# Two inner tiles per SwiGLU step, in-place normalized tiles, a fifth weight buffer and a product moved to VectorE in a two-layer hybrid trunk

## The chip, the cores and the metric

The kernel runs on one core of a Trainium2 chip. The core has TensorE (PE, matrix products, with weight loads listed as PEld), VectorE (DVE), ScalarE (ACT), GpSimd (POOL) and SyncE (SP, which here only issues DMAs). The metric is the device time of one execution in microseconds (us), as the median of several runs.

## The reference

A trunk of two layers over one sequence of 256 positions, 1024 wide. Each layer is a SwiGLU feed-forward part, a mixer, and a second SwiGLU part; layer 0 mixes with RG-LRU and gated linear attention side by side, layer 1 with multi-head latent attention. Every part reads its input through a scale and shift computed from the conditioning vector c, and ends in a gated residual and a layer norm:

```python
def modulate(x, shift, scale):
    return x * (1 + scale[:, None, :]) + shift[:, None, :]

def deepnorm_residual(x, f, gate, g, b, weight=1.0):
    return layer_norm(DN_ALPHA * x + weight * (1 + gate[:, None, :]) * f, g, b)

def swiglu(u, w_in, w_out):
    gate, up = jnp.split(u @ w_in, 2, axis=-1)
    return (jax.nn.silu(gate) * up) @ w_out
...
    # rg_lru
    a = jnp.exp(log_a)
    u = jnp.sqrt(-jnp.expm1(2.0 * log_a)) * (i * x).astype(F32)
    _, h = lax.associative_scan(combine, (a, u), axis=1)
```

The inner width of SwiGLU is 2816, so w_in has 2 x 22 output tiles of 128 (22 gate, 22 up). All arithmetic is f32.

## The kernel before, in words

**Layout and precision.** Activations are kept transposed: a tile is 128 channels by 256 positions, and the 1024 channels are 8 tiles, indexed k. An f32 product is done as three fp32r matmuls on split operands: high·high (L407), low·high (L408) and high·low (L409). The activation u is therefore held as `uhi` and `ulo`, the inner activation of SwiGLU as `hhi` and `hlo`, and each weight as `whi` and `wlo`.

**Weight stream** (class `Stream`). All weight tiles (128x128) lie in the order of their use in slabs of 16 (1 MB). SP brings a slab into one of five `wraw` buffers; the tables of c's projections (`modw`) go through the same buffers. A slab is split in two halves of 8 tiles: ACT copies the half rounded to fp32r (`whi`, L338), DVE subtracts that copy from the raw weights (`wlo`, L339). When PE's program reaches half slab s, the splits up to s + AHEAD have been put into the program; `whi` and `wlo` have four buffers each and AHEAD is 3. One half slab feeds 24 matmuls. The projections of c are sums of products on DVE (`junk`, L388, 144 of them), dispersed among the splits.

**Boundary** (class `Boundary`, six of them, five with a successor). Each output tile of a part gets gate and residual on DVE (`yy`, L581) and its square on ACT; sums over the tiles are kept in `acc`. A correction (`shift`) is made from tile 0 once that is there: ACT rounds it, PE sums it over channels (L566), ACT copies the sum, and POOL subtracts it from seven residual tiles (`ax`, L571). Then mean and variance come from PE (L597 to L600), `center` subtracts the mean from a tile (DVE L603), and r is minus two over the standard deviation. While that runs, PE has the "early" products of the next part's first output tiles with the uncentred input held in two `flat` tiles (two to four output tiles of 8 x 3 matmuls). Then `u(k)` makes the next part's operand of tile k, one tile at a time: DVE multiplies by r (`ut`, L657), ACT adds the shift and rounds (`uhi`, L658), DVE subtracts (`ulo`, L659). Once u is done, `residual` makes the next residual `ax` in two steps, DVE L665 and ACT L666. `u` is called eight times in the first pass over k of the next part, one k per half slab or so.

**SwiGLU** (`ffn`). The first passes take several inner tiles j together over k; after them come the tail j's, one at a time with one bank for the gate and one for the up half. `glu(j)` is: silu on ACT into `sg`, product with the up half on DVE (`h`, L702), split into `hhi` (ACT L444) and `hlo` (DVE L445), each on a 128x256 tile.

**RG-LRU** (`rglru`, called for two groups of four channel tiles). Per tile a small gate weight `rgt` comes by a DMA on SP's queue (L829, two buffers); a convolution, two matmuls (L835, L836) and elementwise work follow, then for the group of four tiles a chain of 128x1024 operations on DVE, of which L850 is the last; POOL multiplies by the input (L851), and DVE runs four scans (L853).

**Order.** A scheduler places each engine's instructions in one fixed order by priorities (`tc.high_priority`) and data; each engine then runs its own list in order, and waits at an instruction whose operands or buffers aren't there.

Of the kernel before, what the change touches and what calls it, by code (L numbers as in the profile page):

```python
# [21 lines left out]
P = 128  # L22
# [32 lines left out]
FROW = 320  # L55
# [176 lines left out]
def trunk_kernel(ctx: ExitStack, tc: tile.TileContext, xT, cvec, pos, wst, modw, colsd,  # L232
# [6 lines left out]
    whi = ctx.enter_context(tc.tile_pool(name="whi", bufs=4))  # L239
# [3 lines left out]
    wlo = ctx.enter_context(tc.tile_pool(name="wlo", bufs=4))  # L243
# [31 lines left out]
    crow = T(wk, [1, DM], tag="junk", bufs=1)  # L275
# [24 lines left out]
    class Stream:  # L300
        RAW = 4
        HS = SLAB // 2
        AHEAD = 3
# [210 lines left out]
    class Boundary:  # L514
        def __init__(self, l, s, weight):
# [14 lines left out]
            if not self.last:  # L530
# [15 lines left out]
                self.ya = [flat(q, F32R).rearrange("p (k c) -> p k c", k=KD) for q in range(2)]  # L546
# [12 lines left out]
        def shift_out(self):  # L559
# [4 lines left out]
            act.activation(yr, y, AF.Copy)  # L564
# [29 lines left out]
        def stats(self, y, ysq):  # L594
# [7 lines left out]
            def center(k):  # L602
                vec.tensor_tensor(self.y[:, k, :], self.y[:, k, :], mean, SUB)  # L603

            odd_next = not self.last and self.next[1] == 1 and self.next[0] % 2
            with tc.high_priority(), tc.manual_schedule(engines={DVE, ACT}):
# [8 lines left out]
                for k in range(PRE):  # L615
                    center(k)
                r, rlast = rsqrt2(v, SEQ)
                self.r = r
                if self.last:
                    for k in range(KD):  # L620
                        self.normal(k, r)
                        if k + PRE < LPOOL:
                            center(k + PRE)
                    return
# [3 lines left out]
            self.center = center  # L628
# [4 lines left out]
            for m, f in early(*self.next):  # L633
                ps = mmps()
                for k in range(KD):
                    mm3(ps[:, :SEQ + 2], W.next((m, k, f)), [t[:, k, :SEQ + 2] for t in self.ya], k == 0, k == KD - 1)
# [7 lines left out]
            if odd_next:  # L644
                for k in range(PRE, KD):
                    center(k)

        def u(self, k):
# [4 lines left out]
            with tc.high_priority(offset=UOFF):  # L653
                if k >= PRE:
                    self.center(k)
                xa = T(wk, [P, SEQ], tag="ut")
                vec.scalar_tensor_tensor(xa, self.y[:, k, :], self.hA[:, k:k + 1], self.r, MULT, MULT)  # L657
                act.activation(uhi[:, k, :], xa, AF.Identity, bias=self.B[:, k:k + 1])  # L658
                vec.scalar_tensor_tensor(ulo[:, k, :], xa, self.B[:, k:k + 1], uhi[:, k, :].bitcast(F32), ADD, SUB)  # L659

        def residual(self, ks=range(KD)):
            W.pause = False
            for k in ks:
                xg = T(wk, [P, SEQ], tag="xh", bufs=3)
                vec.scalar_tensor_tensor(xg, self.y[:, k, :], self.ag[:, k:k + 1], self.r, MULT, MULT)  # L665
                act.activation(ax[:, k, :], xg, AF.Identity, bias=self.ab[:, k:k + 1])  # L666
# [24 lines left out]
    def ffn(l, i, prev):  # L691
        with tc.tile_pool(name=nm("ffn"), bufs=1) as fp:
# [4 lines left out]
            def glu(j, pg, pu, bg=0.0, bu=0.0, off=100):  # L697
                with tc.high_priority(offset=off):
                    sg = T(wk, [P, SEQ], tag="sg")
                    ta(sg, pg, AF.Silu, bias=bg)  # L700
                    h = T(wk, [P, SEQ], tag="h")
                    vec.scalar_tensor_tensor(h, pu, bu, sg, ADD, MULT)  # L702
                    split(h, hhi[:, j, :], hlo[:, j, :])

            for j in range(EARLY if prev else 0):
                (pg, bg), (pu, bu) = prev.values[2 * j:2 * j + 2]
                glu(j, pg, pu, bg, bu)

            passes = ffn_passes(l, i)
            part = {}  # L710
            for g, ks in passes:
                grp = {j: mmps() if q < 6 else axps() for q, j in enumerate(g)}
                for k in ks:
                    prev.u(k) if prev else first_u(k)
                    for j in g:
                        for half in range(2):
                            mm3(grp[j][:, half * SEQ:(half + 1) * SEQ], W.next((m, k, half * NJ + j)), u(k),
                                k == ks[0] and half == 0, k == ks[-1], True)
                if ks[-1] < KD - 1:
                    keep = [flat(q) for q in range(2)]  # L720
                for q, j in enumerate(g):
                    ps = grp[j]
                    if ks[-1] < KD - 1:
                        part[j] = keep[q // 4][:, (q % 4) * 512:(q % 4 + 1) * 512]
                        act.activation(part[j], ps, AF.Copy)
                        continue
                    off = GOFF
                    if j in part:
                        off -= GLATE * q
                        with tc.high_priority(offset=off):  # L730
                            vec.tensor_tensor(part[j], ps, part[j], ADD)  # L731
                        ps = part[j]
                    glu(j, ps[:, :SEQ], ps[:, SEQ:], off=off)
# [582 lines left out]
```

## Time and profile before

| what | value |
|---|---|
| median of 3 runs | 1037.29 us (1035.79 to 1043.17) |
| the profiled execution, its own time | 1033.83 us |
| its span in the profile | 1032.1 us |
| PE busy | 995.5 us, 96% of the span |
| DVE busy | 884.7 us, 86%, 1491 instructions |
| ACT busy | 612.5 us, 59%, 1023 instructions |
| POOL busy | 54.8 us, 5%, 72 instructions |
| granted TensorE clock | 0.996 of full speed |
| moved by DMA | 258.57 MB, mean 251 GB/s |

In a profile line, L339 is line 339 of the kernel; `wlo<-wraw,whi` reads "the tile wlo is made from wraw and whi"; xN counts instructions. A row of a timeline has start, duration, engine, line and operation, and in brackets the idle time before it with what ended that.

### The profile page before, as it was taken

The numbers are of one execution on the slowest core, as the hardware profiler recorded it, in microseconds if no ns is written. First come the engines' busy times: TensorE is split into PE (matmuls) and PEld (weight loads), VectorE is DVE, ScalarE is ACT, GpSimd is POOL, SyncE is SP. The second block draws the span as 40 slices with busy tenths as digits, with TensorE's granted clock in tenths as the row PEclk, the third lists the DMA queues.
The fourth block names the chain that finished last, engine by engine and source line by source line (L and its number), as shares of the span: only waits on it lengthen the run. The fifth ranks groups of instructions, "written<-read, shape, count | busy, mean of one in ns | idle before, by whom it ended". The sixth has DMA issues, their size and how long they took to land.

```text
span 1032.1 us, 20703 instructions
## 1 busy us (share of the span) xinstructions
PE 995.5 (96%) x8338; PEld 972.8 (94%) x8338; DVE 884.7 (86%) x1491; ACT 612.5 (59%) x1023; POOL 54.8 (5%) x72
## 2 busy tenths in 40 slices
PE   6999999999999989999999999999999999999995
PEld 5999999998899979999999999999998889999995
DVE  5789999797998989999998899998888799666664
ACT  4746654567886656745545665455559666545543
POOL 0000010000001020000030000002000200000200
PEclk9999999999999999999999999999999999999998
DMA  9998798554466943699977469898743146665621
GB/s 342 366 339 319 257 368 309 208 204 169 170 264 242 350 185 142 245 361 373 365 279 286 166 251 371 322 359 321 286 167 129 73 164 245 246 224 187 243 83 41
DMA packets 38578, 258.57 MB, mean 251 GB/s; under 512 B 4289, under 2 KB 6849, under 8 KB 7762
## 3 DMA queue, kind: packets, MB, share of 16 engines
q1 hardware_dynamic: 38482, 257.25, 66.7%
q8 instruction: 65, 1.06, 0.4%
q14 instruction: 31, 0.25, 0.1%
HBM read 256.18 MB, written 1.05 MB: 249 GB/s over the span
## 4 chain that ended last, share of the span: by engine, by line
PE 82%; DVE 11%; issue 2%; ACT 2%; DMA 2%; POOL 0%; SPq 0%; DVEq 0%; ACTq 0%
PE mm L409 25%; PE mm L407 25%; PE mm L408 25%; DVE wlo L339 4%; DVE junk L388 2%; DMA wraw<-modw 1%; ACT whi L338 1%; DVE flat L557 1%; DVE yy L581 1%; PE ax L408 1%; PE ax L407 1%; PE ax L409 1%; DVE acc L589 1%; DVE flat L731 0%; DMA rgt<-rgw 0%
## 5 line engine op out<-in xcount | busy, mean ns | idle before, releaser
L339 DVE TENSOR_TENSOR wlo<-wraw,whi 128x1024 fp32r<-128x1024 f32 x340 | 416.7, 1233 | 81.3 <-ACT whi L338 80.8
L338 ACT ACTIVATE whi<-wraw 128x1024 fp32r<-128x1024 f32 x340 | 357.6, 1058 | 212.4 <-PE mm L408 138.0
L407 PE MATMUL mm<-uhi,whi 128*128 128x256 f32 x1672 | 461.4, 278 | 11.5 <-ACT uhi L444 6.0
L409 PE MATMUL mm<-uhi,wlo 128*128 128x256 f32 x1672 | 460.1, 277 | 3.6 <-DVE wlo L339 3.6
L408 PE MATMUL mm<-ulo,whi 128*128 128x256 f32 x1672 | 462.1, 277 | 0.7 <-DVE ulo L445 0.6
L407 PEld LDWEIGHTS mm<-uhi,whi 128*128 128x128 f32 x1672 | 313.6, 188 | 14.9 <-ACT uhi L444 7.9
L409 PEld LDWEIGHTS mm<-uhi,wlo 128*128 128x128 f32 x1672 | 313.8, 188 | 4.2 <-DVE wlo L339 4.1
L408 PEld LDWEIGHTS mm<-ulo,whi 128*128 128x128 f32 x1672 | 314.8, 188 | 1.5 <-DVE ulo L445 1.2
L409 PE MATMUL mm<-hhi,wlo 128*128 128x256 f32 x704 | 194.6, 276 | 1.9 <-DVE wlo L339 1.9
L408 PE MATMUL mm<-hlo,whi 128*128 128x256 f32 x704 | 194.4, 276 | 0.0
L407 PE MATMUL mm<-hhi,whi 128*128 128x256 f32 x704 | 194.3, 276 | 0.0
L388 DVE CUSTOM_DVE_ANT_0 junk<-wraw,cact,cols 128x1024 bf16<-128x1024 f32 x144 | 184.9, 1284 | 5.7 <-DMA wraw<-modw 5.0
L409 PEld LDWEIGHTS mm<-hhi,wlo 128*128 128x128 f32 x704 | 132.1, 188 | 2.3 <-DVE wlo L339 2.3
L407 PEld LDWEIGHTS mm<-hhi,whi 128*128 128x128 f32 x704 | 132.2, 188 | 0.0
L408 PEld LDWEIGHTS mm<-hlo,whi 128*128 128x128 f32 x704 | 132.2, 188 | 0.0
L571 POOL TENSOR_TENSOR ax<-ax,shift 128x256 f32<-128x256 f32 x42 | 42.2, 1039 | 734.7 <-ACT shift L569 734.7
L444 ACT ACTIVATE hhi<-h 128x256 fp32r<-128x256 f32 x88 | 35.9, 413 | 44.3 <-DVE h L702 43.2
L585 ACT ACTIVATE ysq<-yy 128x256 f32<-128x256 f32 x42 | 17.4, 414 | 51.8 <-DVE yy L581 50.0
L702 DVE SCALAR_TENSOR_TENSOR h<-mm,sg 128x256 f32<-128x256 f32 x75 | 30.9, 418 | 7.9 <-PE mm L409 7.9
L581 DVE SCALAR_TENSOR_TENSOR yy<-mm,gate,ax 128x256 f32<-128x256 f32 x48 | 22.8, 478 | 16.2 <-PE mm L409 15.0
L445 DVE TENSOR_TENSOR hlo<-h,hhi 128x256 fp32r<-128x256 f32 x88 | 36.0, 417 | 0.0
L429 ACT ACTIVATE sg<-mm 128x256 f32<-128x256 f32 x75 | 27.4, 366 | 3.0 <-DVE h L702 1.7
(288 smaller groups left out, 1088.1 us busy)
## 6 DMA issues: line engine op xcount, KB each, us to landing
wraw<-wst SPq DMA_DIRECT2D x169, 1024.0 KB, 5.8
wraw<-modw SPq DMA_DIRECT2D x71, 1024.0 KB, 6.5
wraw<-modw SPq DMA_DIRECT2D x2, 512.0 KB, 5.4
yy<-xT SPq DMA_DIRECT2D x8, 128.0 KB, 6.8
wraw<-wst SPq DMA_DIRECT2D x2, 512.0 KB, 7.9
rgt<-rgw SPq DMA_DIRECT2D x8, 128.0 KB, 3.7
outT<-yy SPq DMA_DIRECT2D x3, 256.0 KB, 2.6
outT<-yy SPq DMA_DIRECT2D x2, 128.0 KB, 2.6
```

What stands on the lines that cost most here:

```text
L338: act.activation(hi, raw, AF.Copy)
L339: i = vec.tensor_tensor(lo, raw, hi.bitcast(F32), SUB)
L388: i = vec.tensor_tensor_reduce(junk, t, cact, 1.0, col("mod_b", (l * NMOD + v) * KD + j), MULT, ADD, self.modcols[(l, v)][:, j:j + 1])
L407: pe.matmul(ps, hi, mh, start=start, stop=False, skip_group_check=shared)
L408: pe.matmul(ps, hi, ml, start=False, stop=False, skip_group_check=shared)
L409: pe.matmul(ps, lo, mh, start=False, stop=stop, skip_group_check=shared)
L429: i = act.activation(out, in_, func, **kw)
L444: act.activation(hi, src, AF.Copy)
L445: vec.tensor_tensor(lo, src, hi.bitcast(F32), SUB)
L571: pool.tensor_tensor(ax[:, j, :], ax[:, j, :], shift, SUB)
L581: vec.scalar_tensor_tensor(y, ps, self.gate[:, f:f + 1], ax[:, f, :], MULT, ADD)
L702: vec.scalar_tensor_tensor(h, pu, bu, sg, ADD, MULT)
```

## The change

- **Stream:** AHEAD 3 becomes 4, and `whi` and `wlo` get a fifth buffer. The room comes from smaller `flat` tiles (row 320 to 272, and `ya` cut to the 258 columns that are used) and from the input row `crow`, which now uses a `flat` tile.
- **Boundary:** `center` works on two tiles at once (128x512), and a new `normed` multiplies two tiles by r in place. `u(k)` is then ACT twice from the normed tile with scale and shift by pointers (`uhi` and `ut`), and one DVE subtraction. `residual` is one ACT operation per tile; its DVE step is gone. The rounding of tile 0 for `shift` gets high priority.
- **SwiGLU:** gates of two neighbouring j's share a PSUM bank and their up halves share another, so `glu` runs on 128x512: one silu, one product, one split per pair. The additions of partial sums go by bank. The tail j's go in pairs with 96 matmuls on two banks.
- **RG-LRU:** the product of L851 moves from POOL to DVE, and the `rgt` loads go from SP's queue to ACT's, with three buffers in place of two.
- Some small tiles change their tag, which changes only where they lie.

```diff
-FROW = 320
+FROW = 272
...
-    whi = ctx.enter_context(tc.tile_pool(name="whi", bufs=4))
+    whi = ctx.enter_context(tc.tile_pool(name="whi", bufs=5))
...
-    wlo = ctx.enter_context(tc.tile_pool(name="wlo", bufs=4))
+    wlo = ctx.enter_context(tc.tile_pool(name="wlo", bufs=5))
...
-        AHEAD = 3
+        AHEAD = 4
...
-            act.activation(yr, y, AF.Copy)
+            with tc.high_priority():
+                act.activation(yr, y, AF.Copy)
...
-            def center(k):
-                vec.tensor_tensor(self.y[:, k, :], self.y[:, k, :], mean, SUB)
+            def wide(t, n):
+                return t[:, None, :].broadcast_to([P, n, SEQ])
+
+            def center(k, n=2):
+
+                vec.tensor_tensor(self.y[:, k:k + n, :], self.y[:, k:k + n, :], wide(mean, n), SUB)
+
+            def normed(k, n=2):
+                vec.tensor_tensor(self.y[:, k:k + n, :], self.y[:, k:k + n, :], wide(self.r, n), MULT)
...
             with tc.high_priority(offset=UOFF):
-                if k >= PRE:
-                    self.center(k)
+                if k % 2 == 0:
+                    if k >= PRE:
+                        self.center(k)
+                    self.normed(k)
+                z, a, b = self.y[:, k, :], self.hA[:, k:k + 1], self.B[:, k:k + 1]
                 xa = T(wk, [P, SEQ], tag="ut")
-                vec.scalar_tensor_tensor(xa, self.y[:, k, :], self.hA[:, k:k + 1], self.r, MULT, MULT)
-                act.activation(uhi[:, k, :], xa, AF.Identity, bias=self.B[:, k:k + 1])
-                vec.scalar_tensor_tensor(ulo[:, k, :], xa, self.B[:, k:k + 1], uhi[:, k, :].bitcast(F32), ADD, SUB)
+                act.activation(uhi[:, k, :], z, AF.Identity, bias=b, scale=a)
+                act.activation(xa, z, AF.Identity, bias=b, scale=a)
+                vec.tensor_tensor(ulo[:, k, :], xa, uhi[:, k, :].bitcast(F32), SUB)
...
             for k in ks:
-                xg = T(wk, [P, SEQ], tag="xh", bufs=3)
-                vec.scalar_tensor_tensor(xg, self.y[:, k, :], self.ag[:, k:k + 1], self.r, MULT, MULT)
-                act.activation(ax[:, k, :], xg, AF.Identity, bias=self.ab[:, k:k + 1])
+                act.activation(ax[:, k, :], self.y[:, k, :], AF.Identity, bias=self.ab[:, k:k + 1],
+                               scale=self.ag[:, k:k + 1])
...
-            def glu(j, pg, pu, bg=0.0, bu=0.0, off=100):
+            def glu(j, n, pg, pu, bg=0.0, bu=0.0, off=100):
+
                 with tc.high_priority(offset=off):
-                    sg = T(wk, [P, SEQ], tag="sg")
+                    sg = T(wk, [P, 2 * SEQ], tag="sg")[:, :n * SEQ]
                     ta(sg, pg, AF.Silu, bias=bg)
-                    h = T(wk, [P, SEQ], tag="h")
-                    vec.scalar_tensor_tensor(h, pu, bu, sg, ADD, MULT)
-                    split(h, hhi[:, j, :], hlo[:, j, :])
+                    h = T(wk, [P, 2 * SEQ], tag="h")[:, :n * SEQ]
+                    if n == 1:
+                        vec.scalar_tensor_tensor(h, pu, bu, sg, ADD, MULT)
+                    else:
+                        vec.tensor_tensor(h, pu, sg, MULT)
+                    split(h, *(t[:, j:j + n, :].rearrange("p j s -> p (j s)") for t in (hhi, hlo)))
...
-            for j in range(max(g.stop for g, _ in passes), NJ):
+            j = max(g.stop for g, _ in passes)
+            while j < NJ:
+                n = min(2, NJ - j)
                 pp = [mmps(), mmps()]
-                for half in range(2):
-                    for k in range(KD):
-                        mm3(pp[half][:, :SEQ], W.next((m, k, half * NJ + j)), u(k),
-                            k == 0, k == KD - 1)
-                glu(j, pp[0][:, :SEQ], pp[1][:, :SEQ])
+                for q in range(n):
+                    for half in range(2):
+                        for k in range(KD):
+                            mm3(pp[half][:, q * SEQ:(q + 1) * SEQ], W.next((m, k, half * NJ + j + q)), u(k),
+                                k == 0 and q == 0, k == KD - 1, True)
+                glu(j, n, *(ps[:, :n * SEQ] for ps in pp))
+                j += n
...
-                    rgt = T(ew, [P, 2, P], tag="rgt")
-                    sync.dma_start(rgt, rgw[j])
+                    rgt = T(ew, [P, 2, P], tag="rgt", bufs=3)
+                    act.dma_start(rgt, rgw[j])
...
-                pool.tensor_tensor(tz, tz, xc, MULT)
+                vec.tensor_tensor(tz, tz, xc, MULT)
```

The change also moves instructions on the engines. The rows below are the programs' own order; a row has the line in its own kernel, the operation, and the tiles.

First place, DVE, the end of the first RG-LRU group. Before, the product stands on POOL, between L850 and the scans L853; `bc`, `lb` and `la` belong to the linear attention of the same layer, `xh` to `residual`.

```order
L847 TENSOR_SCALAR ya_496_3169<-ya_496_3169 128x1024
L850 SCALAR_TENSOR_TENSOR ya_495_3168<-ya_495_3168,ya_496_3169 128x1024
L968 TENSOR_TENSOR lb_2980<-lb_2980,mm_3285 128x256
L339 TENSOR_TENSOR wlo_3325<-wraw_3075,whi_3324 128x1024
L853 SCALAR_TENSOR_TENSOR flat_417_2686<-ya_496_3169,ya_495_3168 128x256 x4
L967 TENSOR_TENSOR bc_2981<-bc_2981,mm_3323 128x256
L968 TENSOR_TENSOR lb_2980<-lb_2980,mm_3323 128x256
L665 SCALAR_TENSOR_TENSOR xh_3354<-yy_1821,ag_1849,r_2597 128x256
L339 TENSOR_TENSOR wlo_3363<-wraw_3113,whi_3362 128x1024
```

The same place in the changed kernel, where L883 is the old L850, L884 the product, L886 the scans and L1007 the old L974:

```order
L880 TENSOR_SCALAR ya_470_3101<-ya_470_3101 128x1024
L883 SCALAR_TENSOR_TENSOR ya_469_3100<-ya_469_3100,ya_470_3101 128x1024
L1007 SCALAR_TENSOR_TENSOR la_2911<-mm_3285,la_2911 128x256
L884 TENSOR_TENSOR ya_469_3100<-ya_469_3100 128x1024
L339 TENSOR_TENSOR wlo_3322<-wraw_3063,whi_3321 128x1024
L886 SCALAR_TENSOR_TENSOR flat_391_2617<-ya_470_3101,ya_469_3100 128x256 x4
L1007 SCALAR_TENSOR_TENSOR la_2911<-mm_3316,la_2911 128x256
L339 TENSOR_TENSOR wlo_3353<-wraw_3063,whi_3352 128x1024
```

The product now stands on DVE itself, ahead of a weight split and the scans; the `xh` step and the separate additions to `bc` and `lb` no longer stand between the scans and the next split.

Second place, ACT, the boundary from the first SwiGLU into the layer-0 mixer. `wab` is read off each of the two early products when it ends. Before, the splits of the next part's second and third half slab (`whi_2646`, `whi_2706`) stand here:

```order
L338 ACTIVATE whi_2646<-wraw_2421 128x1024
L639 ACTIVATE wab_2638<-mm_2609 128x2
L658 ACTIVATE uhi_123<-ut_2605,B_1845 128x256
L338 ACTIVATE whi_2706<-wraw_2421 128x1024
L658 ACTIVATE uhi_123<-ut_2734,B_1845 128x256
L639 ACTIVATE wab_2674<-mm_2643 128x2
L658 ACTIVATE uhi_123<-ut_2768,B_1845 128x256
L818 ACTIVATE flat_417_2686<-early_2640,wab_2638 128x256
```

In the changed kernel the second and third half slab are `whi_2577` and `whi_2639`; L674 and L675 are the two steps of `u`, L851 is the old L818:

```order
L338 ACTIVATE whi_2577<-wraw_2317 128x1024
L651 ACTIVATE wab_2571<-mm_2540 128x2
L674 ACTIVATE uhi_123<-yy_1753,B_1777,hA_1785 128x256
L675 ACTIVATE ut_2536<-yy_1753,B_1777,hA_1785 128x256
L651 ACTIVATE wab_2605<-mm_2576 128x2
L675 ACTIVATE ut_2667<-yy_1753,B_1777,hA_1785 128x256
L675 ACTIVATE ut_2700<-yy_1753,B_1777,hA_1785 128x256
L851 ACTIVATE flat_391_2617<-early_2573,wab_2571 128x256
L675 ACTIVATE ut_2734<-yy_1753,B_1777,hA_1785 128x256
L851 ACTIVATE flat_391_2617<-early_2607,wab_2605 128x256
L338 ACTIVATE whi_2639<-wraw_2383 128x1024
```

The split of the third half slab has moved behind the second `wab` and behind seven more operations: three `ut`, two `uhi` (rows like the one shown, left out here), and two L851.

More of the change, by code (lines that the diff above doesn't have):

```diff
@@ L272, in axps @@
         return T(ps_ax, [P, 512], tag="ax")
-    crow = T(wk, [1, DM], tag="junk", bufs=1)
+    crow = T(main, [1, DM], tag="flat0")
     sync.dma_start(crow, cvec)
@@ L545, in __init__ @@
                 self.next = (nl, ns)
-                self.ya = [flat(q, F32R).rearrange("p (k c) -> p k c", k=KD) for q in range(2)]
+                self.ya = [flat(q, F32R)[:, :KD * (SEQ + 2)].rearrange("p (k c) -> p k c", k=KD) for q in range(2)]
                 hi, lo = self.ya
@@ L614, in stats @@
                 vec.tensor_tensor(v, e2, v, SUB)
-                for k in range(PRE):
-                    center(k)
+                if self.last:
+                    for k in range(PRE):
+                        center(k, 1)
+                else:
+                    for k in range(0, PRE, 2):
+                        center(k)
                 r, rlast = rsqrt2(v, SEQ)
@@ L627, in stats @@
                 W.pause = PAUSE
-            self.center = center
+            self.center, self.normed = center, normed
             if not odd_next:
@@ L644, in stats @@
             if odd_next:
-                for k in range(PRE, KD):
-                    center(k)
+                for k in range(0, KD, 2):
+                    if k >= PRE:
+                        center(k)
+                    normed(k)
         def u(self, k):
```

46 lines of the change are left out of this document (28 added, 18 removed).

## The prediction

> **What bounds the kernel now.** First the page: the span, the engines, the chain of what ended last.
>
> ```profile
> span 1032.1 us, 20703 instructions
> ...
> PE 995.5 (96%) x8338; PEld 972.8 (94%) x8338; DVE 884.7 (86%) x1491; ACT 612.5 (59%) x1023; POOL 54.8 (5%) x72
> ...
> PE 82%; DVE 11%; issue 2%; ACT 2%; DMA 2%; POOL 0%; SPq 0%; DVEq 0%; ACTq 0%
> ```
>
> PE is on the chain for 82% and DVE for 11%. A busy share of 96% doesn't say whether PE issues as fast as it can, so the next view is a table by windows: from:to, length, and for each engine busy time and in brackets instructions (PE, PEld, DVE, ACT, POOL), then clock, DMA share, GB/s.
>
> ```profile
> 0.00:40.00 40.00, 29.41 (x203) 26.14 (x204) 25.86 (x43) 21.48 (x34) 1.41 (x14) 1.00 0.93 361
> 40.00:60.00 20.00, 20.00 (x179) 20.00 (x178) 15.99 (x23) 11.15 (x17) 0.00 (x0) 1.00 0.94 331
> 120.00:140.00 20.00, 18.96 (x167) 18.76 (x166) 20.00 (x33) 12.46 (x20) 0.00 (x0) 1.00 0.90 333
> 160.00:180.00 20.00, 18.11 (x156) 17.72 (x156) 20.00 (x44) 10.76 (x17) 0.00 (x0) 1.00 0.83 314
> 260.00:280.00 20.00, 17.48 (x149) 17.04 (x148) 19.63 (x30) 16.61 (x28) 2.40 (x1) 1.00 0.43 158
> 340.00:360.00 20.00, 18.94 (x167) 18.75 (x166) 18.66 (x35) 14.58 (x26) 0.00 (x0) 1.00 0.96 353
> 600.00:620.00 20.00, 20.00 (x179) 20.00 (x178) 20.00 (x37) 14.78 (x28) 0.00 (x0) 1.00 0.66 244
> ```
>
> A full window holds 179 matmuls, 0.112 us each; the 24 matmuls of a half slab then take 2.68 us. In such a window nothing that DVE or ACT saves shortens the kernel: at 600 DVE is full for all 20 us and PE misses nothing. The windows that fall short are where time can be won, and the list of PE's waits (engine, line, what it waited for; total us, times, longest) says for what:
>
> ```profile
> PE mm L409 <- DVE wlo L339: 6.5, 6, 1.5
> PE mm L407 <- ACT uhi L444: 6.0, 1, 6.0
> PE mm L407 <- DVE yy L581: 3.1, 2, 1.9
> PE mm L407 <- ACT whi L338: 2.2, 2, 1.4
> PE ax L597 <- DVE acc L588: 1.3, 1, 1.3
> PE ax L1176 <- ACT pT L1169: 1.1, 1, 1.1
> PE ax L598 <- DVE acc L589: 0.7, 1, 0.7
> ```
>
> So the change can win little: 6.5 us where PE waits for split weights, 6.2 us (3.1 + 1.3 + 1.1 + 0.7) for other work, and 8.2 us (6.0 + 2.2) at the start, before u and the first weights exist. Of 1032 us, 12.7 lie behind the start.
>
> **The weight splits, the main term.** The six waits of 6.5 us are about 1.1 us each. They fall in the windows above at 120 (one), 160 (two) and 260 (two), and 340 (one). In each DVE is full or nearly so (20.00, 20.00, 19.63, 18.66) and the split comes too late. The timeline of DVE shows the two at 260, in the layer-0 mixer, and that of POOL the product of that group:
>
> ```profile
> 269.09 1.22 DVE L850 SCALAR_TENSOR_TENSOR ya<-ya,ya 128x1024 f32<-128x1024 f32 x1
> ...
> 270.56 3.31 DVE L339 TENSOR_TENSOR wlo<-wraw,whi 128x1024 fp32r<-128x1024 f32 x1
> 273.80 2.43 DVE L853 TENSOR_TENSOR_SCAN flat<-ya,ya 128x256 f32<-128x256 f32 x4
> ...
> 276.79 0.47 DVE L665 SCALAR_TENSOR_TENSOR xh<-yy,ag,r 128x256 f32<-128x256 f32 x1
> 277.18 1.21 DVE L339 TENSOR_TENSOR wlo<-wraw,whi 128x1024 fp32r<-128x1024 f32 x1
> ```
>
> ```profile
> 270.39 2.40 POOL L851 TENSOR_TENSOR ya<-ya 128x1024 f32<-128x1024 f32 x1 [61.11 <-DVE ya L850]
> ```
>
> The split at 270.56 takes 3.31 us beside POOL's 2.40 us product, against 1.21 us for the next one: 2.1 us lost on DVE. From 269.09 to the end of the second split (278.39) are 9.3 us. With the product on DVE the row order gives: L883 1.22, product 1.22 (as L850, a 128x1024 operation on two inputs), L1007 twice at about 0.41 (estimated by the 128x256 rows below), split 1.21, scans 2.43, split 1.21: 8.1 us, 1.2 less, though one more product runs on DVE. The Trainium skill ("SBUF — State Buffer", section on the two separate sides) has a rule for it: VectorE with two SBUF inputs and GpSimd take a shared port pair as an exclusive lock, and the loser stops for the whole instruction; by that rule the split would have taken up to 1.21 + 2.40 = 3.61 us, and the trace's 3.31 is near it. By the rule's full stop DVE would win 0.3 us more here, 1.5 in place of 1.2.
>
> The groups of instructions give what else DVE saves (us in total, mean ns of one, idle before):
>
> ```profile
> L339 DVE TENSOR_TENSOR wlo<-wraw,whi 128x1024 fp32r<-128x1024 f32 x340 | 416.7, 1233 | 81.3 <-ACT whi L338 80.8
> L445 DVE TENSOR_TENSOR hlo<-h,hhi 128x256 fp32r<-128x256 f32 x88 | 36.0, 417 | 0.0
> L702 DVE SCALAR_TENSOR_TENSOR h<-mm,sg 128x256 f32<-128x256 f32 x75 | 30.9, 418 | 7.9 <-PE mm L409 7.9
> L665 DVE SCALAR_TENSOR_TENSOR xh<-yy,ag,r 128x256 f32<-128x256 f32 x40 | 17.9, 475 | 0.0
> L659 DVE SCALAR_TENSOR_TENSOR ulo<-ut,B,uhi 128x256 fp32r<-128x256 f32 x32 | 15.2, 476 | 0.2
> L657 DVE SCALAR_TENSOR_TENSOR ut<-yy,hA,r 128x256 f32<-128x256 f32 x32 | 15.2, 476 | 0.0
> L731 DVE TENSOR_TENSOR flat<-mm,flat 128x512 f32<-128x512 f32 x6 | 4.0, 681 | 0.0
> ```
>
> Wide operations: two narrow ones have 2 x 0.418 = 0.84 us, a wide one 0.68 (L731), so by durations a pair saves 0.16 for h and again for hlo. Some 37 pairs of each give up to 12 us. Residual: 40 operations of 0.475, 18 to 19 us by duration, gone. u: two scalar operations at 0.476 become half a wide one (0.34) and a subtraction at 0.417, 0.2 us for each of 32: 6 us. The product costs 2 x 1.22 = 2.4 us. In all at most 35 us of DVE's 884.7. Nearly all of it stands in windows like that at 600, where it hides behind PE and is worth nothing; it counts only as far as it makes the late splits earlier. The fifth buffer acts there too: a split may stand one half slab further ahead, and a burst of DVE work may last one split (1.2 us) or, where DVE then had room, a half slab (2.68 us) longer before PE runs dry. Each wait is some 1.1 us, so one split of credit about covers a single one (120, 340); the two at 160 lie in a window of full DVE, where there is one credit for two waits, and the 0.16 us of a few pairs. I take 5 of the 6.5 us: all at 260 and 120, the better part of those at 340 and 160. Bounds: 2.5 (the place at 260 and little else) to 6.5.
>
> **Other waits.** yy (3.1 us) waits behind POOL's additions at the boundary, which stay; acc, pT and the rest sit behind small operations that the change leaves in place. A lighter DVE and one half slab in reserve help a little: 1 us, between 0 and 3.
>
> **The start.** The three first `rgt` loads now stand at the head of ACT's program. The chain there (start, us):
>
> ```profile
> 2.09 6.32 DMA wraw<-modw
> ...
> 8.54 1.28 DVE junk L388
> ...
> 25.37 1.05 ACT whi L338
> ...
> 32.52 1.05 ACT whi L338
> ```
>
> The first product of c waits for this transfer, and PE's first real matmul for that product; the two waits for `whi` (2.2 us) are the last two rows. Three loads of 128 KB are 393 KB; at the window's 361 GB/s they take 1.1 us. They cost that if they all go ahead of it, and 0 if they stay behind: I take 0.5. The Trainium skill's page "Trainium Kernel Development and Optimization" (Key Constraints) speaks against this edit: DMAs of all issuing engines run on the same 16 DMA engines and interleave, another queue saves only issue time. By that the start would pay towards the 1.1, and the sum below would be 0.6 less gain; that the old queue held no `rgt` here is all the trace can say. In the mixer, moving them past SP's slabs has its gain inside the term of 260.
>
> **u and residual on ACT.** The nearest rows for ACT:
>
> ```profile
> L338 ACT ACTIVATE whi<-wraw 128x1024 fp32r<-128x1024 f32 x340 | 357.6, 1058 | 212.4 <-PE mm L408 138.0 <-issue 37.0 <-DMA wraw<-wst 14.6
> L658 ACT ACTIVATE uhi<-ut,B 128x256 fp32r<-128x256 f32 x32 | 16.0, 505 | 9.3 <-DVE ut L657 8.9
> L830 ACT ACTIVATE ya<-flat,cols 128x256 f32<-128x256 f32 x8 | 4.6, 591 | 3.4 <-DVE flat L853 3.3
> ```
>
> L830 has scale and bias by pointers, as the two steps of the new u have: 0.59 each. Per k ACT then has 1.06 + 2 x 0.59 = 2.24 us in the first pass of a part, against PE's 2.68: it fits, with 0.44 us to spare. The latency of one u grows from 0.48 + 0.51 + 0.48 = 1.46 to 0.68 + 2 x 0.59 + 0.42 = 2.28 us. The early matmuls (two times 2.68 us) cover the first u, and each later one stands ahead of its use. Tight is the boundary into the mixer, where the third half slab's split moved behind the second `wab`:
>
> ```profile
> 209.01 1.07 ACT L338 ACTIVATE whi<-wraw 128x1024 fp32r<-128x1024 f32 x1 [0.63 <-PE mm L408]
> ...
> 210.38 0.15 ACT L639 ACTIVATE wab<-mm 128x2 f32<-128x2 f32 x1
> ```
>
> Before it started at 209.01. Now: 210.38 + 0.15, five u steps at 0.59 and two L851 at 0.50 give 214.5, the rounded copy is there at 215.5 and the split at 216.8. PE ends the second early product at 210.4 and two half slabs at 215.7. So the split is 1.1 us late by durations, and in time if ACT's operations overlap by 0.1 to 0.15 us each: 0.3, between 0 and 1.1.
>
> **Sum.** -5.0 - 1.0 + 0.5 + 0.3 = -5.2 us, between -9.5 (-6.5 - 3.0) and -0.3 (-2.5 + 1.1 + 1.1). From the profiled execution's 1033.83 that is 1028.6. The median of the runs, 1037.29, is 3.46 us above the profiled one; I carry that over, and predict 1032.
>
> **Rivals.**
> - *More than the splits.* All 12.7 us behind the start go, since a lighter DVE shifts every late step, and the two waits for `whi` at the start (2.2 us) too: -12.7 to -14.9, 1022 to 1025. For it: in all short windows DVE is full. Against: POOL's additions, the attention and the start keep their work. Chance 0.23.
> - *Nothing won.* The waits move: the third half slab (1.1), other bursts of wide operations, the start (1.1) eat what the splits give, or DVE's savings all fall into full windows. 1035 to 1040. For it: 600:620. Chance 0.20.
> - *Slower: the ping-pong of u.* ACT waits for `normed`, and its second step for DVE's subtraction two k's back, since `ut` has two buffers; all `whi` splits stand behind a waiting u on ACT, and DVE's splits wait for them. If no early matmul and no reserve covers it, each of 32 u's puts 2.28 - 1.46 = 0.82 us on the path, 26 us: 1032 + 26 = 1058. Half of them exposed gives 1045. It decides once ACT has over 0.44 us of other work per k, such as a residual step (0.59) or silu in the first pass. Against: 212.4 us of ACT's idle time lie before `whi`, mostly waiting for PE to free a buffer, so splits run early. Chance 0.12.
>
> **How the numbers follow.** My forecast has the other 0.45, with a range of 1027.8 to 1037. A measurement of this kernel tells about 1% from no change, so faster means below 1026.9 and slower above 1047.7. Faster: the second case (0.23) and a little of the first, 0.26. Slower: most of the last, 0.11. The rest, 0.63, lies between. The range of 1022 to 1042 leaves out the fourth case and the edges of the second and third.
>
> **What would show it.** PE's waits for `wlo` fall from six to one or two, with 260:280 near 179 matmuls; splits beside no POOL product all near 1.21 us. At the start PE's first matmuls come up to 1.1 us later. After each boundary `whi` follows u without PE waiting more than 1 us. DVE falls to about 850 us, ACT rises by some 10 to 20 us, and the span hardly follows. I am wrong if PE waits for uhi or ulo after a boundary, if the wlo waits stay although DVE is lighter, or if full windows hold other than 179 matmuls.

## The result, and the profile after

The changed kernel takes 1045.68 us (median of 14 runs) beside 1037.12 us of the kernel before (14 runs): a ratio of 1.009, with a 95% interval of 1.0073 to 1.0108. The change makes the kernel slower by 0.9%, where 0.5% faster was forecast, and 1045.68 lies above the stated range of 1027.8 to 1037 us. The profiled execution took 1042.8 us, the shortest of the 14; its span is 1041.1 us.

The page of the changed kernel, in the lines that answer to those shown of before:

```profile
span 1041.1 us, 20372 instructions
...
PE 999.7 (96%) x8338; PEld 975.9 (94%) x8338; DVE 861.3 (83%) x1339; ACT 619.3 (59%) x973; POOL 49.4 (5%) x70
...
PE 65%; DVE 16%; DMA 9%; issue 5%; ACT 4%; POOL 1%; SPq 0%; DVEq 0%; ACTq 0%
```

DVE has 23 us less to do (861.3 for 884.7), and yet its share of the chain grows from 11% to 16%, and that of DMA from 2% to 9%. PE's waits say what became of the places that the prediction counted:

```profile
PE mm L407 <- ACT uhi L444: 6.1, 2, 5.9
PE ax L567 <- ACT shift L565: 4.7, 3, 2.1
PE mm L407 <- DVE yy L582: 3.1, 2, 1.9
PE mm L407 <- ACT whi L338: 2.6, 2, 1.4
...
PE mm L409 <- DVE wlo L339: 2.1, 2, 1.9
...
PE mm L407 <- ACT hhi L444: 1.3, 1, 1.3
...
PE mm L408 <- DVE ulo L676: 1.0, 3, 0.4
```

The waits for `wlo` fell from 6.5 us to 2.1, as forecast. New are the waits for `shift` (4.7 us), `hhi` and the `ulo` of u (L676). DVE's own waits hold the largest change, one line of each list, before first:

```profile
DVE junk L388 <- DMA wraw<-modw: 5.0, 6, 1.3
```

```profile
DVE junk L388 <- DMA wraw<-modw: 35.5, 25, 3.9
```

DVE now stands 35.5 us, in 25 waits, before a product of c whose `modw` tile hasn't landed. To see where that reaches PE, the next table sets the start of PE's N-th matmul in each trace against before (us; minus is earlier; "pin64" and the others are experiments below):

```
   N   before    after  ahead4-  a_oldu  a_oldu_sp  a_rgt_sp  a_pin64  a_pin64_sp
                        alone
 200     39.7    +1.27    +0.35   +0.46      -0.02     -0.18    +0.20       -0.58
2200    291.4    -0.56    -0.69   +0.86      -1.78     -1.24    +0.59       -1.61
2400    318.3    +0.05    +0.05  +10.76      +0.48     -1.36    +1.17       -1.75
4000    509.4    -0.86    -0.12   +9.00      +0.20     -2.32    +0.23       -2.73
4200    532.1    +4.56    -0.12   +9.00      +0.20     -0.84    +0.23       -2.73
5600    692.2    +5.53    -0.16   +8.96      +0.16     -0.23    +0.91       -2.05
5800    714.9    +7.75    -0.16   +8.96      +0.16     +4.97    +0.91       -2.05
6600    818.6    +7.30    -0.16   +9.04      +0.20     +4.48    +0.39       -2.51
6800    845.4    +8.94    -0.21   +9.24      +0.16     +6.01    +2.02       -0.98
8200   1004.1    +8.95    -0.21   +9.24      +0.16     +6.01    +2.04       -0.98
```

Up to the 4000th matmul the changed kernel is ahead by 0.9 us in spite of a later start. Then it loses 5.4 us within 200 matmuls, 2.2 us near the 5700th and 1.6 us near the 6700th. The first is the end of the second SwiGLU of layer 0. DVE's timeline of the changed kernel there:

```profile
513.55 0.68 DVE L722 TENSOR_TENSOR h<-mm,sg 128x512 f32<-128x512 f32 x1
518.04 1.28 DVE L388 CUSTOM_DVE_ANT_0 junk<-wraw,cact,cols 128x1024 bf16<-128x1024 f32 x1 [3.81 <-DMA wraw<-modw]
...
519.25 0.69 DVE L445 TENSOR_TENSOR hlo<-h,hhi 128x512 fp32r<-128x512 f32 x1
519.86 1.22 DVE L339 TENSOR_TENSOR wlo<-wraw,whi 128x1024 fp32r<-128x1024 f32 x1
...
523.33 0.42 DVE L720 SCALAR_TENSOR_TENSOR h<-mm,sg 128x256 f32<-128x256 f32 x1
...
526.13 1.28 DVE L388 CUSTOM_DVE_ANT_0 junk<-wraw,cact,cols 128x1024 bf16<-128x1024 f32 x1 [0.91 <-DMA wraw<-modw]
...
531.02 0.48 DVE L582 SCALAR_TENSOR_TENSOR yy<-mm,gate,ax 128x256 f32<-128x256 f32 x1
```

In the kernel before, the last `h` and the `yy` stand here:

```profile
516.27 0.42 DVE L702 SCALAR_TENSOR_TENSOR h<-mm,sg 128x256 f32<-128x256 f32 x1 [0.53 <-PE mm L409]
...
523.81 0.48 DVE L581 SCALAR_TENSOR_TENSOR yy<-mm,gate,ax 128x256 f32<-128x256 f32 x1
```

A product of c, the 93rd, stands ahead of the urgent work in the changed kernel. DVE is idle from 514.2 to 518.0 for its transfer, and `hlo`, a split, the last `h` and at last the boundary's `yy` come late behind it; `shift` needs that `yy`. Between 518 and 536 PE waits 1.3 us for `hhi`, 0.6 for `hlo` and 2.1 for `shift`. The chain of waits shows why the transfer is late:

```profile
510.07 1.28 DVE junk L388
511.39 6.52 DMA wraw<-modw
518.04 1.28 DVE junk L388
...
521.14 4.97 DMA wraw<-modw
```

The tile could only be asked for at 511.39, when an earlier product had left its raw buffer, and took 6.52 us to land. In the kernel before, PE has no gap in the same stretch and no product of c waits there; its windows for 500 to 520, 520 to 540 and 700 to 720 are full:

```profile
500.00:520.00 20.00, 20.00 (x179) 20.00 (x178) 17.36 (x26) 11.83 (x17) 0.00 (x0) 1.00 0.94 356
520.00:540.00 20.00, 20.00 (x179) 20.00 (x178) 18.48 (x25) 9.54 (x13) 8.24 (x7) 1.00 0.70 270
700.00:720.00 20.00, 20.00 (x178) 20.00 (x178) 17.82 (x25) 9.87 (x14) 7.32 (x7) 1.00 0.90 354
```

### The profile page after: what moved, and what is told of

Same layout as the page of the kernel before. It is cut to its first block, busy times and chain, and to the rows that moved or that the text cites. A ratio compares the mean times of both kernels' runs of the same rounds, so it can differ in the third digit from the quotient of the medians.

```text
span 1041.1 us, 20372 instructions
## 1 busy us (share of the span) xinstructions
PE 999.7 (96%) x8338; PEld 975.9 (94%) x8338; DVE 861.3 (83%) x1339; ACT 619.3 (59%) x973; POOL 49.4 (5%) x70
## 4 chain that ended last, share of the span: by engine, by line
PE 65%; DVE 16%; DMA 9%; issue 5%; ACT 4%; POOL 1%; SPq 0%; DVEq 0%; ACTq 0%
PE mm L408 20%; PE mm L409 20%; PE mm L407 20%; DMA wraw<-modw 7%; DVE wlo L339 5%; DVE junk L388 4%; ACT whi L338 2%; POOL ax L572 1%; DMA rgt<-rgw 1%; DMA wraw<-wst 1%; DVE yy L608 1%; DVE flat L557 0%; DVE yy L582 0%; DVE acc L590 0%; PE mm L1182 0%
## 5 line engine op out<-in xcount | busy, mean ns | idle before, releaser
L338 ACT ACTIVATE whi<-wraw 128x1024 fp32r<-128x1024 f32 x340 | 353.1, 1055 | 164.6 <-PE mm L408 126.2
L388 DVE CUSTOM_DVE_ANT_0 junk<-wraw,cact,cols 128x1024 bf16<-128x1024 f32 x144 | 184.8, 1283 | 36.4 <-DMA wraw<-modw 35.5
L444 ACT ACTIVATE hhi<-h 128x512 fp32r<-128x512 f32 (+1 forms) x47 | 28.0, 600 | 68.3 <-DVE h L722 58.9
L445 DVE TENSOR_TENSOR hlo<-h,hhi 128x512 fp32r<-128x512 f32 (+1 forms) x47 | 30.3, 649 | 0.0
L407 PE MATMUL mm<-flat,whi 128*128 128x258 f32 x96 | 28.7, 299 | 0.0
L408 PE MATMUL mm<-flat,whi 128*128 128x258 f32 x96 | 28.4, 296 | 0.0
```

The source lines that it names most:

```text
L338: act.activation(hi, raw, AF.Copy)
L388: i = vec.tensor_tensor_reduce(junk, t, cact, 1.0, col("mod_b", (l * NMOD + v) * KD + j), MULT, ADD, self.modcols[(l, v)][:, j:j + 1])
L407: pe.matmul(ps, hi, mh, start=start, stop=False, skip_group_check=shared)
L408: pe.matmul(ps, hi, ml, start=False, stop=False, skip_group_check=shared)
L444: act.activation(hi, src, AF.Copy)
L445: vec.tensor_tensor(lo, src, hi.bitcast(F32), SUB)
```

## The experiments

Each kernel was timed in five rounds beside the kernel before; ratios are to that.

**First, the look-ahead and the pairs.** The first theory was that one half slab more of look-ahead puts the products ahead of their transfers. Four kernels: the stream part undone, the stream part alone on the kernel before, SwiGLU undone, and the room of the extra split buffers spent on a sixth raw buffer.

```diff
 a_ahead3, on the changed kernel
-        AHEAD = 4
+        AHEAD = 3
-    whi / wlo: bufs=5
+    whi / wlo: bufs=4
 b_ahead4: the reverse on the kernel before, with FROW = 272, crow in a flat tile and ya cut to 258 columns
 a_raw6: a_ahead3, and
-    wraw: bufs=5
+    wraw: bufs=6
 a_glu1: ffn() as in the kernel before, tiles sg and h 256 wide again
```

> The changed kernel with the stream part alone undone: splits three half slabs ahead, whi and wlo in four buffers. Look-ahead theory (one half slab more of look-ahead puts the products of c ahead of their transfers in DVE's fixed order; DVE stops there, and h, hlo and yy behind it come late): DVE's wait for modw falls from 35.5 us to about 5 to 10, PE's stalls of 4.7 us near 522 to 532 and of 2 us near 715 go, the span comes to about 1034 us. Pair theory (the wide SwiGLU steps and paired tail tiles make the bursts and the lateness): the stalls and the 35.5 us stay, span 1040 to 1042.

Measured: 1059.35 us, ratio 1.0214 (1.0184 to 1.0245). DVE's wait for `modw` stays at 36.8 us. The look-ahead theory falls: taking the look-ahead away makes this kernel 14 us slower. Seven waits for `wlo` are back (5.0 us), but more is lost in the mixer (8.2 us between the 2200th and the 2400th matmul, with 3.2 us of waiting for `rgt`) and near 715 (8.5 us).

> The kernel before with the stream part alone: look-ahead 4, five whi and wlo buffers, and the smaller flat tiles that make the room. Look-ahead theory: DVE's wait for modw rises from 5.0 us to 25 or more, PE stalls appear around 520 to 530, span 1034 to 1038 in spite of fewer late splits. Pair theory: no such waits (5 us), two to five of the six wlo waits go, span 1027 to 1031.

Measured: 1033.78 us, ratio 0.9973 (0.9957 to 0.9989). The look-ahead alone is a small gain: waits for `wlo` go from 6.5 us to 1.8, the wait for `modw` stays at 6.1, and there is no stall at 520. In its place PE waits 3.0 us for `la` of the linear attention, one reason why the gain is not larger.

> The changed kernel with the SwiGLU part alone undone: one inner tile per step, tail tiles one by one. Look-ahead theory: the modw wait on DVE stays above 25 us, span 1039 to 1043. Pair theory: it falls below 10 us, stalls at 522 to 532 and 715 go, span about 1033.

Measured: 1042.34 us, ratio 1.0069 (1.0044 to 1.0093). The `modw` wait is still 30.0 us. The loss near 520 is 0.9 us here, but one of 4.6 us stands near 715: the pairs sharpen a stall here and there and don't cause it.

> The changed kernel with look-ahead 3 and four whi and wlo buffers, and the room of those two buffers (8 KB per partition) spent on a sixth raw buffer. Look-ahead theory, in the form that the transfers come too late for the order: modw wait under 5 us, span 1028 to 1033, a little below the same kernel with five raw buffers. Pair theory: stalls stay in part since DVE's bursts stay, span 1038 to 1041.

Measured: 1045.49 us, ratio 1.0093 (1.0065 to 1.0121). Beside a_ahead3, on which it is built, this is 14 us faster, and only 0.1 us is lost near 520 and 2.5 near 715, so room for transfers does count. But the `modw` wait stays at 29.3 us, the kernel is as slow as the changed one, and PE's waits for `wlo` grow to 7.7 us: a lack of room alone isn't the cause.

**What differs.** With both theories down I counted, in the programs' order of DVE, behind how many weight splits each product of c stands. For the 73rd, the 93rd (on which DVE stops near 514), the 105th and the 129th (on which it stops 2.5 us near 703), with DVE's wait for `modw` from the traces (us):

```
                 73rd    93rd   105th   129th   modw wait
before            144     171     205     237       5.0
b_ahead4          145     171     205     237       6.1
after             141     169     202     235      35.5
a_ahead3          141     170     201     235      36.8
a_glu1            141     169     202     235      30.0
a_raw6            140     167     201     233      29.3
a_rgt_sp          141     169     202     235      27.5
a_oldu            144     171     205     236       9.5
a_oldu_sp         144     171     205     236       9.2
a_pin64           145     175     205     241       3.1
a_pin64_sp        145     175     205     241       1.1
```

The a_pin64 rows have the products kept where the program issues them: the 73rd behind the 145th split, the 93rd behind the 175th. Both the kernel before and the changed one issue products by the same lines, and the scheduler may move them up. Before, the 73rd has moved by one split and the 93rd by four; in the changed kernel, with the DVE steps of `residual` and `u` gone, by four and by six. The two splits by which the kernels differ at the 93rd are 5.4 us of PE's time (2.68 us each). The order is fixed when the program is built; on the chip the transfer isn't there yet, and DVE stops. That the scheduler moves a product up because its model finds DVE free is inferred from these counts. That gives the second theory, and two ways to test it: put the DVE steps back, or forbid the move.

```diff
 a_oldu, on the changed kernel: center, u and residual as in the kernel before
 a_pin: in reduce(), for each product i of c
+            if self.split is not None:
+                queue_behind(i, self.split)      # self.split: the last wlo issued
 a_rgtlate: each rgt load ordered behind the last rounding of weights issued
-                    act.dma_start(rgt, rgw[j])
+                    queue_behind(act.dma_start(rgt, rgw[j]), W.rounded)
 a_pin_rgt: both of the last two
```

> The changed kernel with the boundary part alone undone: center on one tile, u and residual with their DVE steps as before (the high priority of tile 0's rounding stays). New theory, order: without those DVE steps the scheduler finds DVE free and moves products of c up to three splits ahead, to where their transfers have not landed; DVE stops there. With the steps back those products stand two or three splits later again, DVE's wait for modw falls from 35.5 us to 10 or less, the stalls near 522 to 532 and 715 go, and the span falls to about 1032 though DVE works some 20 us more. Rival, lateness of u itself (latency of the two ACT steps): the modw wait stays near 30 us, and the gain, if any, lies within 15 us behind each boundary.

Measured: 1044.73 us, ratio 1.0076 (1.0049 to 1.0103). Half as expected: the `modw` wait falls to 9.5 us and the two stalls at 520 and 715 are gone (the table: +9.00 at 4000, +8.96 at 5800), though DVE works 19 us more. But 9.9 us are lost between the 2200th and the 2400th matmul, in the mixer. There PE waits for a gate weight, in PE's list of waits of this kernel:

```profile
PE ax L853 <- DMA rgt<-rgw: 3.6, 1, 3.6
```

and in ACT's timeline the load's issue stands behind the tanh and exp of other tiles, at 301.69, and the next tanh finds ACT idle for 5.60 us:

```profile
301.69 0.34 ACTq L847 DMA_DIRECT2D rgt<-rgw  x1
...
302.82 2.02 ACT L338 ACTIVATE whi<-wraw 128x1024 fp32r<-128x1024 f32 x2
310.44 0.47 ACT L429 ACTIVATE sg<-ax,hba 128x256 f32<-128x256 f32 x1 [5.60 <-PE ax L854]
```

Not all of the 9.9 us is waiting. Behind this wait the granted clock is about half for 6.8 us, as two windows of this kernel show, and PE then waits another 1.9 us for ACT's `yy`:

```profile
308.00:312.00 4.00, 3.33 (x13) 3.07 (x14) 0.43 (x1) 1.56 (x4) 0.00 (x0) 0.63 0.97 401
312.00:316.00 4.00, 4.00 (x21) 4.00 (x21) 2.26 (x3) 2.59 (x3) 0.00 (x0) 0.52 0.31 131
```

> The changed kernel with one thing more: each product of c is ordered behind the split that the program issued last before it, so the scheduler may not move it ahead. Order theory: nothing else changes, DVE's wait for modw falls below 10 us, the stalls at 522 to 532 and 715 go, the span falls by 6 to 8 us to 1033 to 1035. Rival (DVE's lighter load or the wide steps are themselves at fault): the span stays at 1040. It may also fail in another way: a product later than before holds its raw buffer longer, and weight transfers wait (wlo waits on PE over 5 us).

Measured: 1050.74 us, ratio 1.0137 (1.0111 to 1.0164). The `modw` wait is 0.3 us and nothing is lost at 520 or 715 (+14.55 at the 4200th matmul, +15.23 at the 5800th). But at the start, where the first u waits for these products, PE is 10.0 us behind the kernel before at the 200th matmul (it waits 15.3 us for `uhi`), and 7.7 us go in the mixer, with 2.6 us of waiting for `rgt`.

> The changed kernel with the rgt loads still on ACT's queue, but each ordered behind the rounding of weights issued before it, so none stands at the program's start. If the three loads cost the start 1.25 us: PE's 200th matmul returns from 40.9 to 39.7 us and the span falls by 1.0 to 1.3 us. If the start is later for another reason (the input row in a flat tile, the fifth buffer): no change at the start.

Measured: 1042.27 us, ratio 1.0047 (1.0022 to 1.0071). The start is 1.5 us earlier than in the changed kernel (-0.19 for +1.27 at the 200th matmul). The profiled run still has the other losses, larger there than in the changed kernel's (4.4 us near 520, 6.1 near 715).

> Both edits together, products of c kept behind their splits and rgt loads not at the start. Order theory: the gains add, 7 to 9 us below the changed kernel, span 1031 to 1034, about the time of the kernel before or a little less. Rival: 1039 to 1041.

Measured: 1048.76 us, ratio 1.0116 (1.0088 to 1.0144): PE is 6.6 us behind at the 200th matmul here, so the sum that was expected wasn't to be had with this form of the rule.

**The clean forms.** The rule without the start, the old boundary with `rgt` on SP, and `rgt` on SP alone:

```diff
 a_pin64: a_pin, but only behind the mixer of layer 0
-            if self.split is not None:
+            if self.split is not None and self.nconv > 130:
 a_pin64_sp, a_oldu_sp, a_rgt_sp: a_pin64, a_oldu and the changed kernel with
-                    rgt = T(ew, [P, 2, P], tag="rgt", bufs=3)
-                    act.dma_start(rgt, rgw[j])
+                    rgt = T(ew, [P, 2, P], tag="rgt")
+                    sync.dma_start(rgt, rgw[j])
```

> The changed kernel with the products of c ordered behind their splits, but only once 130 half slabs are split, behind the mixer of layer 0; up to there the order is the changed kernel's. Order theory: DVE's modw wait falls below 10 us, the 5.4 us near 522 to 532 and the 2.2 us near 715 go, nothing is added at the start or in the mixer, span 1032 to 1035. Rival, the lighter DVE and the wide steps are at fault, or late products hold raw buffers: span 1039 or more.

Measured: 1033.95 us, ratio 0.9979 (0.9965 to 0.9992). One rule on the order takes some 11 us off the changed kernel by the medians, with all of its parts still in; the two profiled executions, 1042.8 and 1035.9 us, differ by 6.9 us. DVE's timeline at the place of the stall:

```profile
516.32 1.28 DVE L390 CUSTOM_DVE_ANT_0 junk<-wraw,cact,cols 128x1024 bf16<-128x1024 f32 x1
...
517.53 0.42 DVE L724 SCALAR_TENSOR_TENSOR h<-mm,sg 128x256 f32<-128x256 f32 x1
517.86 1.28 DVE L390 CUSTOM_DVE_ANT_0 junk<-wraw,cact,cols 128x1024 bf16<-128x1024 f32 x1
...
519.07 0.42 DVE L449 TENSOR_TENSOR hlo<-h,hhi 128x256 fp32r<-128x256 f32 x1
519.40 2.36 DVE L340 TENSOR_TENSOR wlo<-wraw,whi 128x1024 fp32r<-128x1024 f32 x2
...
524.05 0.48 DVE L586 SCALAR_TENSOR_TENSOR yy<-mm,gate,ax 128x256 f32<-128x256 f32 x1
```

No product waits here, the last `h` comes at 517.53 instead of 523.33, and `yy` at 524.05 instead of 531.02. The windows of PE say the same, 500 to 520, 520 to 540 and 700 to 720, of the changed kernel and then of this one:

```profile
500.00:520.00 20.00, 20.00 (x179) 20.00 (x178) 15.58 (x21) 9.24 (x12) 0.00 (x0) 1.00 0.72 267
520.00:540.00 20.00, 15.76 (x131) 14.96 (x130) 14.90 (x20) 5.82 (x10) 5.81 (x7) 1.00 0.74 263
700.00:720.00 20.00, 18.30 (x159) 17.95 (x158) 14.76 (x20) 9.09 (x12) 0.61 (x1) 1.00 0.83 324
```

```profile
500.00:520.00 20.00, 20.00 (x179) 20.00 (x178) 18.17 (x31) 12.39 (x16) 0.00 (x0) 1.00 0.86 336
520.00:540.00 20.00, 20.00 (x179) 20.00 (x178) 17.38 (x22) 9.58 (x14) 9.35 (x7) 1.00 0.75 274
700.00:720.00 20.00, 20.00 (x178) 20.00 (x178) 17.38 (x23) 9.97 (x15) 8.66 (x7) 1.00 0.87 322
```

> The same with the rgt loads back on SP's queue with two buffers. If the three loads at the head of the program cost the start: another 1.2 us less at the start. If rgt on ACT's queue is what makes the mixer fragile: no wait of PE for rgt over 1 us. Span 1030 to 1033. Against it: the wait on SP's queue for rgt that the kernel before had on its chain (4.9 us from issue to landing at 261) comes back, 1 to 3 us in the mixer.

Measured: 1033.68 us, ratio 0.9977 (0.9961 to 0.9994), span 1031.1. Fastest of the changed forms by its median, but not told apart from a_pin64 or b_ahead4.

> The changed kernel with boundary steps and rgt loads as before: what is left is the stream, the wide SwiGLU and the product on DVE. Order theory and rgt theory together: modw wait about 10 us or less, no stall of 10 us around 305 and 322, none at 532 and 715, span 1028 to 1032, below the kernel before. If the 10 us in the mixer come from the old u and not from rgt on ACT's queue, they stay: span 1040.

Measured: 1033.80 us, ratio 0.9985 (0.9967 to 1.0002). The 10 us in the mixer are gone (+0.48 at the 2400th matmul for +10.76), so the old u alone doesn't lose them: it takes `rgt` on ACT's queue as well. Nor does that queue always cost so much: the changed kernel, with `rgt` on it too, loses 0.6 us there. No difference from the kernel before can be told.

> The changed kernel with the rgt loads alone back on SP's queue, two buffers. Start 1.2 us earlier. Order theory: the stalls near 520 to 532 and 715 stay, modw wait above 25 us, span 1037 to 1040. If rgt on ACT's queue were behind those stalls too: span 1030 to 1033.

Measured: 1044.21 us, ratio 1.0067 (1.0044 to 1.009). The start is 1.5 us earlier, the `modw` wait is 27.5 us, and the losses at 520 and 715 stay (1.5 and 5.2 us, 6.7 together for 7.6, though shared out otherwise): `rgt` on ACT's queue isn't what makes those.

## Why the prediction was wrong

**The bound** (little to be won, full windows at 178 or 179 matmuls) holds in every kernel; none came under the one before by more than 0.3%. That 1045.68 still lies in the band of 1026.9 to 1047.7 that the prediction counted as no change is luck: the losses that made it weren't in its sum.

**The weight splits**: forecast -5.0 us. The wait falls by 4.4 us. At 120, 260 and 340 it is gone, as forecast; the two at 160 became one of 1.9 us, where the better part had been counted as won. By the 4000th matmul the gain is 2.1 us beside the later start, since PE now also waits 0.9 us for `shift` near 160, 0.9 for `la` in the mixer, and loses 0.6 at the boundary at 209. At 260 the split beside POOL's product is down to 1.22 us, but the product's chain ends later (L883 at 274.01, L850 stood at 269.09), since splits and `lb`, `bc` were put between its steps; that stretch is off PE's path by now.

**Prices of single operations** held: h 0.685 us and `normed` 0.684 (0.681 forecast), the steps of u and residual on ACT 0.591 (0.59). The totals fell short of the forecast: DVE is at 861.3 us (about 850 expected), and ACT rises by 6.8 us (10 to 20 expected).

**The start**: 0.5 was taken, 1.1 was the bound. The three changed forms with `rgt` on SP and the one with it late have the 200th matmul at -0.6 to 0.0 us, those with it at the head of ACT's program (a_pin and its pair aside) at +0.2 to +1.6. With one trace each the groups nearly touch, and b_ahead4, with `rgt` on SP, is at +0.35. So the term is probably real, about 1.1 us between the means of the two groups (b_ahead4 counted with SP), and 1.3 us in the changed kernel's trace; it was too small by half a microsecond or more. The Trainium skill's rule ("Trainium Kernel Development and Optimization", Key Constraints), that queues of all engines share and interleave on the same DMA engines, fits that, and it was the better guide.

**The step that failed** is the one that let DVE's saved time count "only as far as it makes the late splits earlier", else "hides behind PE and is worth nothing". It took DVE's order as given. The scheduler put products of c two or three splits earlier into the freed time (141 for 144 at the 73rd, 169 for 171 at the 93rd), and these waited for their transfers in DVE's fixed order, 35.5 us for 5.0. The traces of the changed kernel give 5.4 us near 520 and 2.2 us near 715; the forecast had nothing there. a_oldu and a_pin64 take these losses away, one by putting DVE work back, the other by the order alone. It could have been seen beforehand: the order shows the products two or three splits earlier, and the prediction looked at DVE's order only where PE had waited.

**The rivals.** The slower rival had the right sign for a wrong reason, and that its half-exposed case says 1045 is luck. Its place, PE waiting for `ulo` behind a boundary, is 1.0 us in three waits. At the tight boundary at 209 the 0.3 us weren't lost where they were forecast: the third half slab's split starts on ACT at 213.55, in time. PE loses some 0.6 us there to the `ulo` of the first u, which the prediction held to be covered by the early matmuls. The term for other waits (-1.0) didn't come: yy's 3.1 us and the acc waits are where they were.

**What stays open.** The sum of the changed kernel's trace by the table is +1.3 (start), -2.1 to the 4000th matmul, +5.4, +1.0 (0.4 right behind 520, and 0.6 at the boundary near 585, which a_pin64 loses too), +2.2, and +1.2 to the end with the 1.6 us near the 6700th matmul, 9 us in all, of which 7.6 are shown by experiment to come from the order of the products; the start's 1.3 come at least in part from `rgt`. The 1.6 us go with the clock, as told below, and not with the order. Why the scheduler places the products ahead of their transfers stays open.

## What to carry to other kernels

When a change takes work off an engine that is not the bottleneck, ask what the scheduler will put into the gap: an in-order engine that runs background work earlier than its data arrives holds up the urgent work behind it. Compare the whole order of that engine, above all where the background work stands against the transfers that feed it, and tie such work to a point in the program where its data is surely there. A DMA issued from a compute engine's queue stands in that engine's order too: at its head it competes with the first transfers (0.2 to 1.6 us at the start here), and in the middle it is issued only when the engine gets there.

## What the runs showed of the hardware

In the changed kernel's trace the granted TensorE clock dropped once in the middle of the run. At the boundary behind the attention PE has gaps of about 1.3 and 0.7 us with two matmuls between them, and these gaps are the same in all 14 kernels, before and after. The clock's record in each trace holds only 1.0 and 0.5, and the points at which it changes lie whole multiples of 3.41 us apart. So one can cut each trace into stretches of 3.41 us at these points. The two around the gaps, after:

```profile
841.20:844.60 3.40, 1.33 (x7) 0.76 (x6) 3.37 (x8) 2.08 (x4) 0.00 (x0) 1.00 0.61 219
844.60:848.00 3.40, 3.40 (x11) 2.55 (x11) 1.44 (x5) 1.48 (x5) 0.00 (x0) 0.50 0.23 94
```

and before:

```profile
832.40:835.80 3.40, 2.07 (x18) 1.90 (x18) 3.37 (x7) 2.44 (x5) 0.00 (x0) 1.00 0.72 284
835.80:839.30 3.50, 2.70 (x13) 1.79 (x14) 2.56 (x6) 2.46 (x6) 0.00 (x0) 1.00 0.43 143
```

After, both gaps lie in one stretch, which has 2.07 us without a matmul; in the next the clock is 0.50 and PE loses 1.6 us. Before, the gaps are shared between two stretches (1.33 and 0.80 us), and the clock stays at 1.00. In the eight traces in which one stretch holds 1.5 to 2.1 us of these gaps, the clock is 0.5 in the next: the changed kernel, a_glu1, a_pin, a_pin_rgt, a_pin64, a_pin64_sp, a_rgt_sp and a_rgtlate. In the other six no stretch holds more than 1.35 us, and it stays at 1.0. So at this place the clock goes with where the same gaps fall in time, which differs from trace to trace; the 1.6 us aren't a cost of the change as such. Elsewhere in the traces the same count doesn't separate the two so cleanly (half clock behind 1.3 us in one place, none behind 1.9 us in two), so no exact limit is shown.
